# A hybrid encoder layer on one core: order within matmul pairs, a 64-byte start, three first blocks at once, splits ahead of other work

## The chip, the core and the metric

The kernel runs on one core of a Trainium2 chip. TensorE (PE) does the matmuls out of SBUF into PSUM; its weight loads are shown apart as PEld. VectorE (DVE), ScalarE (ACT) and GpSimd (POOL) do the elementwise work, and SyncE (SP) issues nearly all DMAs. The metric is the device time of one execution in microseconds (us), and lower is better.

## The reference, cut to what matters

One layer on 256 tokens of width 2048, in float32:

```
hn   = rmsnorm(x) * norm_w
proj = hn @ w_in                       # 2048 x 18432: q v f_fwd f_bwd z_a b_gate c_gate h_b z_b
A: 16 heads of 128, chunks of 64, forward and backward
   f = lb + (1-lb)*sigmoid(f_logit); k = 1-f; gated linear recurrence of silu(q), k, v
   o_a = head_rmsnorm(o_fwd + o_bwd) * silu(z_a)
B: y = b_gate * conv3(c_gate * h_b);  o_b = rmsnorm(y) * silu(z_b)
h  = x + concat(o_a, o_b) @ w_out      # 4096 x 2048
h  = h + (p @ w_ple) * sigmoid(h @ w_ple_gate)      # 256 x 2048, 2048 x 2048
out = rmsnorm(h)
```

Nearly all arithmetic is in the four matrix products, and all weights are read once.

## The kernel before, in words

**Two halves for precision.** Each float32 operand of a large product is split into a high part, rounded to the matmul's own 32-bit format (fp32r), and the rest, the low part. A product is high x high + high x low + low x high. For weights this is `Stream.split` (L69 on ACT casts the high part, L70 on DVE subtracts it for the low part), for the normalised input `x_split` (L228 on ACT, L229 on DVE), which also multiplies by `norm_w`. The factor 1/rms of each token is applied later, to the results.

**Blocks.** The columns of `w_in` are cut into 72 blocks of 256. One block is a sum over 16 k-tiles of 128 rows, and there are four matmuls in a k-tile: two halves m of the output, and for each a *pair*. The long matmul of a pair has the high part as weights and streams high and low of the other operand, 512 columns, into a whole PSUM bank. The short one has the low part as weights and streams the high part, 256 columns, into the first half of the same bank. In k-tile 0 the pair is issued long, short (L284, L285), since the long one also clears the bank; in the 15 others short, long (L287, L288). The evacuation (`evac`, L302/L303 or L307/L308) adds the two halves of the bank. For blocks of q and the gates the weights are the stationary operand and `xs` (the split input) streams; for `z_a` and `v` it is the other way about (`token_major`).

**Order of blocks.** Pairs of heads i = 0 to 7, each with the blocks FF, FB (forget gates), Q, ZA, V; then i = 0 to 7 with CG, HB, BG, ZB for group B; then the product with `w_out` in four column groups, first the half that has `mixa` as stationary operand (`pa`), then that with `mixb` (`pb`), three matmuls of 512 columns for each k-tile and m (L630 to L632); then `w_ple` (`pp`, stationary `pt`) and `w_ple_gate` (`pg`, stationary `ht`), with the same three lines.

**Weights.** `Stream` loads tiles of 1 MB (`raw`, three buffers) over SP and splits them in halves into `spl` tiles (five buffers). `ws.get(i)` splits up to three parts ahead. A part is four k-tiles of a block.

**Start.** SP issues the first loads by hand (L138 for x, L56 for weights). Blocks FF and FB of pair 0 run together, part by part, and their work on ACT, DVE and PE is kept in the order written (`manual_schedule`). Everything else is ordered by Tile's scheduler: at each point an engine gets, among the instructions it takes to be ready, the one with the highest priority, and priority is the order of the program text. So work of DVE that was written earlier goes ahead of a split written later, if both are ready.

**Norms and attention.** Small steps are placed among the matmuls with `at(dt, fn)`, where one tick is one k-tile of a block. After the first blocks the tokens are loaded row by row into `xf32` (L241), squared and summed (L248 on ACT into a bank with tag `kv`, L249 on DVE into one with tag `o`), turned into 1/rms (`x_norms`, L255 to L259) and spread over partitions by two matmuls (`norms_spread`, L264 to L266: `rps`, `rbc`). POOL multiplies gates and q by `rbc` (L312). `mix_pair` then builds, from the gates, the decays of the recurrence: sigmoid and log on ACT (L376, L379, L386), scans and differences on DVE (L390 to L424), exponentials on ACT (L425 to L428), products on DVE (L429, L430) and on POOL (L438 kc and qc, L444 kx). Scores (L459 and `cx`, L501) and outputs (L511, L512) run on PE 20 to 44 ticks after `mix_pair` is written, that is from the fourth k-tile of the next pair's FF on.

**SBUF.** Pools grow from the left (`const`, `raw`, `spl`, `xs`, and later `ht` in the place of `xs`) and from the right end (`mixa`, below it the attention tiles, later `mixb` in their place). The allocator works in steps of 32 bytes.

Of the kernel before, what the change touches and what calls it, by code (L numbers as in the profile page):

```python
# [8 lines left out]
F32 = mybir.dt.float32  # L9
# [8 lines left out]
P = 128  # L18
# [12 lines left out]
class Stream:  # L31


    def __init__(self, nc, rawp, splp, ahead):
        self.nc, self.rawp, self.splp, self.ahead = nc, rawp, splp, ahead
# [15 lines left out]
    def load(self, j, k0=0, k1=None):  # L51
        src, k, n = self.todo[j]
        if j not in self.raws:
            self.raws[j] = self.rawp.tile([P, 2048], F32, tag="raw", name=f"raw{j}")
        dst = self.raws[j][:, : k * n].rearrange("p (k n) -> p k n", n=n)
        self.nc.sync.dma_start(dst[:, k0:k1], src[:, k0:k1])  # L56
# [24 lines left out]
def tile_hymba_encoder(  # L81
# [26 lines left out]
    mctx = ExitStack()  # L108
    mixp = mctx.enter_context(tc.tile_pool(name="mixp", bufs=1, side="right"))
    mixa = mixp.tile([P, NH, 2, T], F32R, name="mixa")  # L110
    actx = ExitStack()
    ap_ = actx.enter_context(tc.tile_pool(name="ap", bufs=1, side="right"))


    ws = Stream(nc, rawp, splp, 3)
# [18 lines left out]

    xf32 = xp.tile([P, NKT, T], F32, name="xf32")
# [20 lines left out]
    dve.memset(wz, 0.0)  # L156
    wps = psm.tile([P, 512], F32, tag="o", name="wps")
# [76 lines left out]
    rx = const.tile([P, 2], F32, name="rx")  # L234
# [5 lines left out]
    def load_tokens():  # L240
        nc.sync.dma_start(xf32.rearrange("p k t -> p (k t)").rearrange("p (m d) -> p m d", m=2), xtok)  # L241
# [30 lines left out]
    def gemm_part(acc, w, g, token_major):  # L272
        for k in range(4):
            kt = 4 * g + k
            for m in range(2):
                a = acc[m].rearrange("p a b -> p (a b)")
                if token_major:
                    lh, ll = xs[:, kt, 0, m * P : (m + 1) * P], xs[:, kt, 1, m * P : (m + 1) * P]
                    rf, rh = w[:, k, :, :].rearrange("p s n -> p (s n)"), w[:, k, 0, :]
                else:  # L280
                    lh, ll = w[:, k, 0, m * P : (m + 1) * P], w[:, k, 1, m * P : (m + 1) * P]
                    rf, rh = xs[:, kt, :, :].rearrange("p s n -> p (s n)"), xs[:, kt, 0, :]
                if kt == 0:
                    pe.matmul(a, lhsT=lh, rhs=rf, start=True, stop=False)  # L284
                    pe.matmul(a[:, :T], lhsT=ll, rhs=rh, start=False, stop=False)  # L285
                else:
                    pe.matmul(a[:, :T], lhsT=ll, rhs=rh, start=False, stop=False)  # L287
                    pe.matmul(a, lhsT=lh, rhs=rf, start=False, stop=(kt == NKT - 1))  # L288
            tick()
# [25 lines left out]
    ids2 = [blocks[c, 0] for c in (B_FF, B_FB)]  # L315
    acc2 = [acc_in(c, 0) for c in (B_FF, B_FB)]
    with tc.manual_schedule(engines={ENG.Activation, ENG.DVE, ENG.PE}):
        for g in range(4):
            for c in range(2):
                half, v = ws.open(ids2[c][g])  # L320
                if g == 0 and c == 0:
                    for q in range(2):
                        x_split(2 * q)
                        ws.split(half[:, 2 * q : 2 * q + 2], v[:, 2 * q : 2 * q + 2])
                        x_split(2 * q + 1)
                else:
                    if g:
                        x_split(4 * g + 2 * c)
                        x_split(4 * g + 2 * c + 1)
                    ws.split(half, v)  # L330
            for c in range(2):
                gemm_part(acc2[c], ws.parts[ids2[c][g]], g, False)
# [190 lines left out]
    for i in range(8):  # L523
        xf = ap_.tile([P, 2, 2, T], F32, tag="xf", name=f"xf{i}", bufs=2)
        evac(acc2[0] if i == 0 else gemm_in(B_FF, i, False), lambda m: xf[:, 0, m, :], ap_)
        evac(acc2[1] if i == 0 else gemm_in(B_FB, i, False), lambda m: xf[:, 1, m, :], ap_)
        qt = ap_.tile([P, 2, T], F32, tag="qt", name=f"qt{i}")
        evac(gemm_in(B_Q, i, False), lambda m: qt[:, m, :], ap_)
# [61 lines left out]
    rb = const.tile([P, 2], F32, name="rb")  # L590
# [76 lines left out]
    rf = const.tile([P, 2], F32, name="rf")  # L667
    dummy = const.tile([P, 2], F32, name="dummy")
# [118 lines left out]
```

## Time and profile before

| | |
|---|---|
| median of 3 runs | 1159.03 us (1158.61 to 1160.16) |
| the profiled execution | 1158.74 us, span 1157.0 us |
| granted PE clock, mean | 0.995 |
| PE busy | 1142.3 us in 6832 instructions |
| splits on DVE (L70) | 389 instructions, 522.3 us |
| splits on ACT (L69) | 389 instructions, 405.0 us |
| DMA | 214.29 MB, mean 185 GB/s |

The page gives for each engine its busy time and its share of the span. The chain of waits follows the work that ended last back from the last instruction, at each step to what released it. Rows of groups give line, engine, operation, tiles, shape, count, then busy time and mean duration in ns, then the idle time of the engine before them and what ended it. Rows of the timeline give start, duration, engine, line, operation, and in brackets the idle time before and its releaser. Rows of stretches give the busy time of each engine with the number of instructions that touch the stretch, then the granted clock, the DMA share and the GB/s. Ends of matmuls are modelled, so the pace of PE is read from the number of matmuls in a stretch, not from their mean duration.

### The profile page before, as it was taken

The numbers are of one execution on the slowest core, as the hardware profiler recorded it, in microseconds if no ns is written. First come the engines' busy times: TensorE is split into PE (matmuls) and PEld (weight loads), VectorE is DVE, ScalarE is ACT, GpSimd is POOL, SyncE is SP. The second block draws the span as 40 slices with busy tenths as digits, with TensorE's granted clock in tenths as the row PEclk, the third lists the DMA queues.
The fourth block names the chain that finished last, engine by engine and source line by source line (L and its number), as shares of the span: only waits on it lengthen the run. The fifth ranks groups of instructions, "written<-read, shape, count | busy, mean of one in ns | idle before, by whom it ended". The sixth has DMA issues, their size and how long they took to land.

```text
span 1157.0 us, 16851 instructions
## 1 busy us (share of the span) xinstructions
PE 1142.3 (99%) x6832; PEld 981.4 (85%) x6832; DVE 763.6 (66%) x949; ACT 639.9 (55%) x889; POOL 234.8 (20%) x167
## 2 busy tenths in 40 slices
PE   8999999999999999999999999999999999999997
PEld 7878888888888888888888888888888888888886
DVE  6687777685958585966666666676666545545554
ACT  6767576666758584855544444444444334434554
POOL 1232414151414041331221221121210000000121
PEclk9999999999999999999999999999999999999999
DMA  8754545454544555455555555555557555555541
GB/s 284 301 175 153 183 163 196 152 183 146 198 167 159 174 177 181 152 178 182 183 187 184 198 191 187 182 182 184 187 190 262 183 198 180 191 204 196 197 166 74
DMA packets 31614, 214.29 MB, mean 185 GB/s; under 512 B 3504, under 2 KB 3888, under 8 KB 7088
## 3 DMA queue, kind: packets, MB, share of 16 engines
q1 hardware_dynamic: 31392, 213.14, 53.6%
q8 instruction: 53, 0.87, 0.3%
q14 instruction: 25, 0.20, 0.1%
q10 hardware_dynamic: 144, 0.08, 0.0%
HBM read 211.11 MB, written 2.10 MB: 184 GB/s over the span
## 4 chain that ended last, share of the span: by engine, by line
PE 93%; DVE 2%; DMA 2%; POOL 1%; ACT 1%; SPq 0%; issue 0%; ACTq 0%; DVEq 0%
PE a L288 41%; PE a L287 21%; PE a L284 3%; PE pa L630 3%; PE pb L630 3%; PE pb L631 3%; PE pb L632 3%; PE pa L631 3%; PE pa L632 3%; PE pg L630 3%; PE pg L631 3%; PE pg L632 3%; PE a L285 1%; DVE spl L70 1%; PE scps L459 1%; PE cx L501 1%
## 5 line engine op out<-in xcount | busy, mean ns | idle before, releaser
L70 DVE TENSOR_TENSOR spl<-raw,spl 128x1024 fp32r<-128x1024 f32 (+1 forms) x389 | 522.3, 1348 | 305.9 <-ACT spl L69 304.9
L288 PE MATMUL a<-xs,spl 128*128 128x512 f32 x1680 | 597.2, 398 | 0.0
L69 ACT CAST spl<-raw 128x1024 fp32r<-128x1024 f32 (+1 forms) x389 | 405.0, 1045 | 343.0 <-PE a L288 193.7
L287 PE MATMUL a<-xs,spl 128*128 128x256 f32 x1680 | 476.0, 283 | 0.5 <-DVE spl L70 0.3
L288 PEld LDWEIGHTS a<-xs,spl 128*128 128x128 f32 x1680 | 316.7, 189 | 73.0
L287 PEld LDWEIGHTS a<-xs,spl 128*128 128x128 f32 x1680 | 318.1, 189 | 3.7 <-DVE spl L70 1.3
L288 PE MATMUL a<-spl,xs 128*128 128x512 f32 x480 | 171.4, 401 | 2.2 <-DVE spl L70 2.2
L287 PE MATMUL a<-spl,xs 128*128 128x256 f32 x480 | 135.4, 282 | 0.0
L288 PEld LDWEIGHTS a<-spl,xs 128*128 128x128 f32 x480 | 91.0, 190 | 24.1 <-DVE spl L70 2.5
L287 PEld LDWEIGHTS a<-spl,xs 128*128 128x128 f32 x480 | 91.4, 190 | 0.7
L307 ACT COPY r<-a 128x256 f32<-128x256 f32 x112 | 40.6, 372 | 47.4 <-PE a L288 46.8
L691 POOL TENSOR_TENSOR hh<-hh,fw 128x512 f32<-128x512 f32 (+1 forms) x10 | 12.8, 1293 | 264.5 <-PE pp L632 245.0
L630 PE MATMUL pg<-spl,ht 128*128 128x512 f32 (+1 forms) x160 | 55.7, 348 | 0.0
L632 PE MATMUL pg<-spl,ht 128*128 128x512 f32 (+1 forms) x160 | 55.5, 347 | 0.0
L631 PE MATMUL pg<-spl,ht 128*128 128x512 f32 (+1 forms) x160 | 55.5, 347 | 0.0
L630 PE MATMUL pa<-spl,mixa 128*128 128x512 f32 x128 | 51.2, 400 | 0.0
L438 POOL TENSOR_TENSOR qc<-pf,ge 128x256 f32<-128x256 f32 x16 | 43.9, 2748 | 34.4 <-DVE pf L430 34.4
L631 PE MATMUL pb<-spl,mixb 128*128 128x512 f32 x128 | 50.6, 395 | 0.0
L630 PE MATMUL pb<-spl,mixb 128*128 128x512 f32 x128 | 50.6, 395 | 0.0
L632 PE MATMUL pb<-spl,mixb 128*128 128x512 f32 x128 | 50.6, 395 | 0.0
L631 PE MATMUL pa<-spl,mixa 128*128 128x512 f32 x128 | 50.6, 395 | 0.0
L632 PE MATMUL pa<-spl,mixa 128*128 128x512 f32 x128 | 50.6, 395 | 0.0
(174 smaller groups left out, 1233.7 us busy)
## 6 DMA issues: line engine op xcount, KB each, us to landing
raw<-in_w_in_dram SPq DMA_DIRECT2D x140, 1024.0 KB, 5.0
raw<-in_w_out_dram SPq DMA_DIRECT2D x32, 1024.0 KB, 4.9
raw<-in_w_gate_dram SPq DMA_DIRECT2D x12, 1024.0 KB, 4.9
raw<-in_w_gate_end_dram SPq DMA_DIRECT2D x4, 1024.0 KB, 4.9
raw<-in_w_in_dram SPq DMA_DIRECT2D x7, 512.0 KB, 8.4
xf<-in_xtok_dram SPq DMA_DIRECT2D x1, 2048.0 KB, 9.9
hh<-in_xtok_dram SPq DMA_DIRECT2D x1, 2048.0 KB, 8.8
raw<-in_w_ple_dram SPq DMA_DIRECT2D x4, 512.0 KB, 3.5
```

Of the source, the lines that this page charges most:

```text
L69: self.nc.scalar.copy(out=v[:, :, 0, :], in_=r)
L70: self.nc.vector.tensor_tensor(out=v[:, :, 1, :], in0=r, in1=v[:, :, 0, :], op=ALU.subtract)
L284: pe.matmul(a, lhsT=lh, rhs=rf, start=True, stop=False)
L285: pe.matmul(a[:, :T], lhsT=ll, rhs=rh, start=False, stop=False)
L287: pe.matmul(a[:, :T], lhsT=ll, rhs=rh, start=False, stop=False)
L288: pe.matmul(a, lhsT=lh, rhs=rf, start=False, stop=(kt == NKT - 1))
L307: act.copy(out=r, in_=acc[m][:, 1, :])
L438: pool.tensor_tensor(out=c64(dst[:, d]), in0=c64(src[:, d, :, half * P : (half + 1) * P]), in1=g.unsqueeze(3).broadcast_to([P, 2, 2, CH]), ...
L630: pe.matmul(acc[m], lhsT=lh, rhs=w[:, k, 0, :], start=(kt == 0), stop=False)
L631: pe.matmul(acc[m], lhsT=lh, rhs=w[:, k, 1, :], start=False, stop=False)
L632: pe.matmul(acc[m], lhsT=ll, rhs=w[:, k, 0, :], start=False, stop=(kt == nk - 1))
L691: pool.tensor_tensor(out=h, in0=h, in1=fw[:, cs], op=ALU.mult)
```

## The change

1. *Pairs.* `gemm_part` issues long, short in every k-tile.
2. *A start on 64 bytes.* `mixa` gets 8 more elements per partition (32 bytes) and is used without them; all that lies below it on the right side moves by 32 bytes. Four small constants (`rx`, `rb`, `rf`, `dummy`) become slices of one tile `few`.
3. *Three first blocks.* FF, FB and Q of pair 0 run together. Q's sums stand in the banks with tags `kv` and `tr`. The first four k-tiles come in pieces of 1, 1 and 2 k-tiles: loads, splits and matmuls. Second halves of the three weights (tiles `raw1`, `raw3`, `raw5`) go into a pool of their own, `rawx`, in the place where `mixa` is put later. A dummy activation at the start comes ahead of the first real one on ACT. The tokens come in two loads, and the norms' steps at 6 to 14 ticks after the first blocks in place of 18 to 31.
4. *Splits first.* In `get`, splits are issued with a priority as if they were written 300 instructions earlier.

```diff
@@ Stream
+    def load(self, j, k0=0, k1=None, pool=None):
...
+            tag = f"raw{j}" if pool else "raw"
+            self.raws[j] = (pool or self.rawp).tile([P, 2048], F32, tag=tag, name=f"raw{j}")
...
     def get(self, i):
         while self.next <= min(i + self.ahead, len(self.where) - 1):
             if self.next not in self.parts:
-                self.split(*self.open(self.next))
+                part = self.open(self.next)
+                with self.tc.high_priority(offset=300):
+                    self.split(*part)
@@ start
-    mixa = mixp.tile([P, NH, 2, T], F32R, name="mixa")
...
+    rawx = rctx.enter_context(tc.tile_pool(name="rawx", bufs=1, side="right"))
...
+    few = const.tile([P, 16], F32, name="few")
+    rx, rb, rf, dummy = (few[:, 2 * j : 2 * j + 2] for j in range(4))
...
-    load_x(0, 2)
     nc.scalar.dma_start(vec, vecs)
-    ws.load(0, 0, 2)
-    load_x(2, 4)
-    ws.load(0, 2, 4)
-    ws.load(2, 0, 4)
+    PIECES = ((0, 1), (1, 2), (2, 4))
+    for k0, k1 in PIECES:
+        load_x(k0, k1)
+        for c in range(3):
+            ws.load(2 * c, k0, k1)
     for g in range(1, 4):
         load_x(4 * g, 4 * g + 4)
-        for c in range(2):
-            ws.load(2 * c + g // 2, 4 * (g % 2), 4 * (g % 2) + 4)
+        for c in range(3):
+            ws.load(2 * c + g // 2, 4 * (g % 2), 4 * (g % 2) + 4, rawx if g > 1 else None)
...
+    act.activation(dummy[:, 0:1], wz[:, 0:1], AF.Copy)
@@ gemm_part
-                if kt == 0:
-                    pe.matmul(a, lhsT=lh, rhs=rf, start=True, stop=False)
-                    pe.matmul(a[:, :T], lhsT=ll, rhs=rh, start=False, stop=False)
-                else:
-                    pe.matmul(a[:, :T], lhsT=ll, rhs=rh, start=False, stop=False)
-                    pe.matmul(a, lhsT=lh, rhs=rf, start=False, stop=(kt == NKT - 1))
+                pe.matmul(a, lhsT=lh, rhs=rf, start=(kt == 0), stop=False)
+                pe.matmul(a[:, :T], lhsT=ll, rhs=rh, start=False, stop=(kt == NKT - 1))
@@ first blocks
-    ids2 = [blocks[c, 0] for c in (B_FF, B_FB)]
-    acc2 = [acc_in(c, 0) for c in (B_FF, B_FB)]
+    first = (B_FF, B_FB, B_Q)
+    ids3 = [blocks[c, 0] for c in first]
+    acc3 = [acc_in(c, 0) for c in first[:2]]
+    acc3.append([psm.tile([P, 2, T], F32, tag=t, name=f"a{B_Q}_0_{m}") for m, t in enumerate(("kv", "tr"))])
     with tc.manual_schedule(engines={ENG.Activation, ENG.DVE, ENG.PE}):
         for g in range(4):
...
+            parts = [ws.open(ids3[c][g]) for c in range(3)]
+            for k0, k1 in PIECES if g == 0 else ((0, 4),):
+                for k in range(k0, k1):
+                    x_split(4 * g + k)
+                for half, v in parts:
+                    ws.split(half[:, k0:k1], v[:, k0:k1])
+                for c in range(3):
+                    gemm_part(acc3[c], parts[c][1], g, False, k0, k1)
+    rctx.close()
+    mctx = ExitStack()
+    mixp = mctx.enter_context(tc.tile_pool(name="mixp", bufs=1, side="right"))
+    mixa = mixp.tile([P, NH * 2 * T + 8], F32R, name="mixa")[:, : NH * 2 * T]
...
-    at(2, load_tokens)
+    for m in range(2):
+        at(2 + m, lambda m=m: load_tokens(m))
     for c in range(4):
-        at(18 + 2 * c, lambda c=c: x_squares(c))
-    at(27, x_norms)
-    at(31, norms_spread)
+        at(6 + c, lambda c=c: x_squares(c))
+    at(11, x_norms)
+    at(14, norms_spread)
```

More of the change, by code (lines that the diff above doesn't have):

```diff
@@ L232, in x_split @@
         )
-    rx = const.tile([P, 2], F32, name="rx")
     rbc = const.tile([P, T], F32, name="rbc")
@@ L270, in acc_in, with gemm_part @@
         return [psg.tile([P, 2, T], F32, tag="g", name=f"a{c}_{i}_{m}") for m in range(2)]
-    def gemm_part(acc, w, g, token_major):
-        for k in range(4):
+    def gemm_part(acc, w, g, token_major, k0=0, k1=4):
+        for k in range(k0, k1):
             kt = 4 * g + k
@@ L312, in by_norms @@
         pool.tensor_tensor(out=t, in0=t, in1=r.unsqueeze(1).broadcast_to([P, n, T]), op=ALU.mult)
-    ids2 = [blocks[c, 0] for c in (B_FF, B_FB)]
-    acc2 = [acc_in(c, 0) for c in (B_FF, B_FB)]
+    first = (B_FF, B_FB, B_Q)
+    ids3 = [blocks[c, 0] for c in first]
+    acc3 = [acc_in(c, 0) for c in first[:2]]
+    acc3.append([psm.tile([P, 2, T], F32, tag=t, name=f"a{B_Q}_0_{m}") for m, t in enumerate(("kv", "tr"))])
     with tc.manual_schedule(engines={ENG.Activation, ENG.DVE, ENG.PE}):
         for g in range(4):
[L319 to L332, printed above, removed]
+            parts = [ws.open(ids3[c][g]) for c in range(3)]
+            for k0, k1 in PIECES if g == 0 else ((0, 4),):
+                for k in range(k0, k1):
+                    x_split(4 * g + k)
[7 more added lines that the diff above has]
+    mixa = mixp.tile([P, NH * 2 * T + 8], F32R, name="mixa")[:, : NH * 2 * T]
+    mixa = mixa.rearrange("p (k s t) -> p k s t", k=NH, s=2)
+    actx = ExitStack()
+    ap_ = actx.enter_context(tc.tile_pool(name="ap", bufs=1, side="right"))
     at(1, lower_bounds)
-    at(2, load_tokens)
+    for m in range(2):
+        at(2 + m, lambda m=m: load_tokens(m))
     for c in range(4):
-        at(18 + 2 * c, lambda c=c: x_squares(c))
-    at(27, x_norms)
-    at(31, norms_spread)
+        at(6 + c, lambda c=c: x_squares(c))
+    at(11, x_norms)
+    at(14, norms_spread)
     def c64(t):
```

26 lines of the change are left out of this document (9 added, 17 removed).

## The prediction

> **What bounds the kernel now.** I read the page first (busy times, chain of waits), then the busy time by stretches, then the timeline of the first 75 us.
>
> ```profile
> span 1157.0 us, 16851 instructions
> PE 1142.3 (99%) x6832; PEld 981.4 (85%) x6832; DVE 763.6 (66%) x949; ACT 639.9 (55%) x889; POOL 234.8 (20%) x167
> PE 93%; DVE 2%; DMA 2%; POOL 1%; ACT 1%; SPq 0%; issue 0%; ACTq 0%; DVEq 0%
> ```
>
> PE is busy for 99% and carries 93% of the chain. Time can go only where PE waits, where its clock is low, or where the same matmuls follow each other more slowly than they could. Stretches show the first two (columns: stretch, its length, busy time and count of PE, PEld, DVE, ACT, POOL, then granted clock, DMA share, GB/s):
>
> ```profile
> 0.00:7.00 7.00, 4.10 (x21) 3.94 (x21) 1.75 (x7) 2.46 (x4) 3.47 (x18) 1.00 0.67 181
> 7.00:32.50 25.50, 24.90 (x128) 20.56 (x129) 20.19 (x35) 18.65 (x30) 0.00 (x0) 0.93 0.91 334
> 32.50:43.90 11.40, 11.40 (x68) 9.95 (x68) 7.91 (x18) 8.05 (x17) 1.47 (x3) 1.00 0.83 348
> 43.90:55.20 11.30, 11.30 (x68) 10.01 (x67) 7.77 (x10) 7.17 (x10) 4.87 (x2) 1.00 0.80 275
> 55.20:70.30 15.10, 12.89 (x65) 10.97 (x64) 12.67 (x24) 13.85 (x21) 5.29 (x5) 0.89 0.21 73
> ```
>
> The first two blocks (FF and FB of pair 0) end at 32.5, Q at 43.9, ZA at 55.2, V at 70.3. A block is 64 matmuls; V takes 15.1 us, 3.8 more than ZA, at a clock of 0.89. The third kind shows in stretches of PE alone:
>
> ```profile
> 549.69:560.79 11.10, 11.10 (x65) 1.00 0.54 190
> 560.79:572.09 11.30, 11.30 (x66) 1.00 0.54 187
> 594.66:865.54 270.88, 270.88 (x1538) 1.00 0.55 187
> 97.76:131.40 33.64, 33.64 (x193) 1.00 0.51 173
> 918.00:958.00 40.00, 40.00 (x173) 1.00 0.54 184
> 1056.00:1096.00 40.00, 40.00 (x178) 1.00 0.57 197
> ```
>
> Rows 1 and 2 are neighbouring blocks of the same work: 11.10 and 11.30 us, without a wait. Row 3 is 24 blocks at 11.29, row 4 three blocks at 11.21. So one instruction stream has two paces, 347 and 353 ns for a pair of matmuls. Rows 5 and 6 hold only 512-column matmuls, with weights from `mixa`/`mixb` and from `ht`/`pt`; with some two counted at the edges, 40/171 = 234 ns and 40/176 = 227 ns.
>
> **The change, part by part.**
>
> *Padding of mixa.* The 8 extra elements move `mixa` down by 32 bytes, and all that lies below it on that side (`mixb`, the attention tiles). By the tile sizes, in the allocator's steps of 32 bytes, `mixa` and `mixb` start 32 past a multiple of 64 today, `ht` and `pt` on one; after it all four start on one. The moving operand, `spl`, and the shape are the same in rows 5 and 6, so the start of the weights is the candidate for the 7 ns. There are 6 x 128 such matmuls (L630 to L632, `pa` and `pb`, each x128): 768 x 6.7 ns = 5.1 us, all on the path. Bounds 0 to -5.1; I take -5.1, because both stages hold their pace throughout.
>
> Against it speaks the Trainium skill, TensorE: Matmul & The Clock Gate, Step-by-step: what each phase is for: loading the next weights takes no SBUF read bandwidth from the running matmul. By that rule the term is 0 and the forecast 1151; the two rows above do not show that it holds here, but they do not isolate the start address either.
>
> The shared `few` tile makes the other side 64 bytes shorter: `raw`, `spl`, `xs` and `ht` move, and stay on multiples of 64. I cost that at nothing; if starts on 128 mattered, all matmuls would pay, and no row shows one with such a start.
>
> *Long then short.* Today k-tile 0 goes long, short and the others short, long, so a block ends long, the next begins long, and two shorts meet after k-tile 0. Afterwards lengths alternate without a break over all blocks. Matmuls and weight loads are the same in number. The pace changed from 11.10 to 11.30 exactly at a block boundary (560.79), with nothing else on PE, and stayed for the 27 blocks to 865.54. Where no boundary disturbs it, a fast pace could last: 27 x (11.29 - 11.10) = 5 us there, and 21 blocks (Q, ZA, V of seven pairs, row 4) x some 0.15 = 3 us, with a little more in FF and FB: up to -9. If the even alternation locks at the slow pace, the fast ones lose 0.2 each: of 72 blocks 27 and 21 are slow, 14 hold attention matmuls, so some ten, up to +2. The attention matmuls still interrupt and can start either pace, so I take the middle, -4.
>
> *The first three blocks.* Today:
>
> ```profile
> 4.53 1.28 ACT L228 ACT_TABLE_LOAD   x1 [4.53 <-DMA xf<-in_xt_dram]
> 4.65 0.19 DVE L197 TENSOR_TENSOR mx<-vec 128x32 f32<-128x32 f32 x1 [3.00 <-DMA vec<-in_vecs_dram]
> 7.00 0.47 PE L284 MATMUL a<-xs,spl 128*128 128x512 f32 x1 [1.78 <-DVE xs L229]
> 6.46 9.34 SPq L56 DMA_DIRECT2D raw<-in_w_in_dram  x2
> 15.84 0.43 SPq L138 DMA_DIRECT2D xf<-in_xt_dram  x1
> 3.13 8.27 DMA xf<-in_xt_dram
> 4.00:8.00 4.00, 2.07 (x12) 0.99 0.96 263
> 8.00:12.00 4.00, 3.66 (x15) 0.58 1.00 381
> L228 ACT ACTIVATE xs<-xf,vec 128x256 fp32r<-128x256 f32 x16 | 7.4, 501 | 0.2
> L229 DVE SCALAR_TENSOR_TENSOR xs<-xf,vec,xs 128x256 fp32r<-128x256 f32 x16 | 7.1, 480 | 1.2 <-ACT xs L228 1.2
> ```
>
> The dummy activation takes the table load (1.28) out of the wait at 4.53, but `vec`, which x_split also reads, lands only at 4.6. The split of x on ACT and DVE (0.50 and 0.48) puts the first matmul at 5.7, 1.3 earlier. SP issues 24 loads in place of 14, some 0.45 us each by the row at 15.84, done by some 12 us, and no longer stands from 6.5 to 15.8 for a raw buffer, since `rawx` holds the second halves; the weights of ZA and the tokens behind them on SP find it free. Bytes now bind: per k-tile x and three weights, 0.52 MB for 6 x 0.35 = 2.1 us of PE (250 GB/s, against 381 moved at 8 to 12). But the first bytes come slowly: the x load issued at 3.13 landed at 11.4, and with it, in SP's order, 2.1 MB, just k-tiles 0 to 3 of the new order. FF's piece of k-tiles 2 and 3 (1.6 MB) would be there near 10.2 and split by 11.5; 3 x 1.4 us of matmuls end at 15.7, not at 5.7 + 8.4 = 14.1. FF's weights for k-tiles 4 to 7 (3.1 MB, 381 GB/s) land near 14 and are split (ACT 1.05, DVE 1.35, with x in between) by 16.8. Idle together 2.7 us. Three blocks need 3 x 11.1 = 33.3: 5.7 + 2.7 + 33.3 = 41.7, against 43.9. With half the clock somewhere (0.58 at 8 to 12 today) 43.3, with no idle time 39.5. I take -2; bounds -4.4 to 0.
>
> A rule against this part is in the Trainium skill, DMA: Bandwidth & Descriptors, How a descriptor splits into AXI transactions: a descriptor that doesn't start on 256 bytes costs a transaction more, and the shift by 64 takes `raw` and `xf32` off such starts. As an estimate by that page a 1 KB piece then needs 5 for 4, which would take half of these 2 us (forecast 1147), while 8 KB rows lose 3% of a DMA share of 0.54.
>
> *Splits first.* The stall in V:
>
> ```profile
> 36.00 0.70 DVE L249 SCALAR_TENSOR_TENSOR xk<-xf 128x512 f32<-128x512 f32 x1 [1.18 <-DMA xf<-in_xtok_dram]
> 41.31 0.36 DVE L259 COPY rw<-rx 128x128 f32<-128x128 f32 x2
> L264 PE MATMUL rps<-ident,rw 128*128 128x128 f32 x3 | 0.5, 274 | 0.0
> 63.55 0.27 PE L287 MATMUL a<-spl,xs 128*128 128x256 f32 x1
> 66.04 0.80 PE L288 MATMUL a<-spl,xs 128*128 128x512 f32 x1 [2.21 <-DVE spl L70]
> 57.59 0.41 DVE L390 TENSOR_SCALAR xf<-xf,noml,oml 128x256 f32<-128x256 f32 x1 [3.84 <-ACT lf L386]
> 64.76 2.35 DVE L70 TENSOR_TENSOR spl<-raw,spl 128x1024 fp32r<-128x1024 f32 x2
> 50.04 2.63 POOL L312 TENSOR_TENSOR xf<-xf,rbc 128x1024 f32<-128x1024 f32 x1 [9.31 <-DVE rbc L265]
> 72.49 1.91 POOL L444 TENSOR_TENSOR kx<-kc,ge 128x512 f32<-128x512 f32 x1
> 74.45 0.71 PE L501 MATMUL cx<-qc,kx 128*128 128x128 f32 x4 [0.47 <-POOL kx L444]
> L70 DVE TENSOR_TENSOR spl<-raw,spl 128x1024 fp32r<-128x1024 f32 x387 | 520.9, 1352 | 304.8 <-ACT spl L69 303.7
> L69 ACT CAST spl<-raw 128x1024 fp32r<-128x1024 f32 x387 | 403.8, 1047 | 341.8 <-PE a L288 193.7 <-PE pb L632 56.1 <-PE pa L632 47.1
> 126.06 1.05 POOL L444 TENSOR_TENSOR kx<-kc,ge 128x512 f32<-128x512 f32 x1
> 134.76 0.30 PE L459 MATMUL scps<-qc,dd 128*32 128x128 f32 x2
> ```
>
> From 57.6 to 64.8 DVE works on the gates of pair 0 while V's next split waits; PE stands 2.2 us and then runs at half clock: with the clock 4.0 us in all (15.1 - 11.1). Splits ahead of that work end it: -4.0. What is late next is the chain that starts when `rbc` is spread (xf scaled at 50.04) and ends with kx at 74.4, 24.4 us later; today PE arrives just then (0.47). Afterwards PE would be there at 41.9 + 25 = 67 in program order. The chain does not start earlier: the squares of x write into bank `kv`, now held by Q's accumulator until its evacuation after 42. From the squares to `rw` it took 5.7 us today (36.0 to 41.7); with splits between, and `rps` on PE, rbc comes at 50 to 52. More splits (up to 8 x 1.35 for 3 today) then lie within the chain. PE can pass the time with FF of pair 1 if the scheduler orders it so. I net this place at -2; bounds -4 (it does) and +9 (below). For later pairs kx is done at 127 and used at 134.8, 7.7 us of slack against a few splits: nothing. Evacuations wait behind one split, 1.35, of the block of 11 us that PSUM leaves them: nothing. Tokens in two loads: one issue more, hidden.
>
> **Sum.** -5.1 - 4 - 2 - 2 = -13.1 on the profiled execution, 1158.74 us (span 1157.0 and 1.7 around it), 0.3 under the median 1159.03: 1145.6 by its own time, 1146 against the median.
>
> **Rivals.** (1) *The chain to the first scores becomes the bound.* rbc at 52.2, 24.4 us of chain and five more splits, 6.8, give kx at 83.4; PE, if it holds the scores in program order, stands 16 us and one low-clock window, 1.7, follows: 10.4 later than 74.7. With padding -5.1 and order 0, 1164. For it speaks that POOL and DVE already end just in time; against it, that `rps` (L264) ran before 43.9, ahead of ZA's matmuls that the program lists first, so PE's order is not fixed. It decides from kx later than 82 (74.7 + 5.1 + 2.3) where the pace brings nothing.
> (2) *The order brings nothing:* the attention matmuls put PE in the slow pace as before: 1150; with the ten fast blocks lost, 1152. The stretch at 97.76 speaks for it.
> (3) *The padding does nothing* (the pace of `pa` has another cause): 1151.
> (4) *The fast pace holds throughout and V's stall goes whole:* 1159 - 5.1 - 9 - 2 - 4 = 1139.
>
> **How the numbers follow.** Forecast 0.35 (its own range 1142 to 1149), (2) 0.25, (4) 0.15, (1) 0.10, (3) 0.08, between (1) and no change 0.07. Below 1136 lies only (4) with the startup's best end, above 1157 only (1) and its neighbours. 0.2%, 2.3 us, is about what a measurement of this kernel can tell from no change: faster 0.83, same 0.07, slower 0.10.
>
> **What would show it.** `pa` and `pb` at 227 ns spacing (178 in 40 us); blocks at 11.1 us; first matmul by 5.7 and Q's end near 42; V at 11.1 us with no clock below 1 after 12 us; a wait of PE at the first scores under 3 us. I am wrong if PE shows a long wait on POOL kx or DVE before the first scores, if `pa` stays at 173 in 40 us, or if all blocks take 11.3.

## The result, and the profile after

The changed kernel takes 1146.9 us (median of 4 runs, 1145.79 to 1148.26) against 1159.6 us for the kernel before on the same chip (1158.61 to 1160.17). The ratio is 0.9895, with a 95% interval of 0.9883 to 0.9907. The forecast was 1146. The profiled execution took 1148.26 us, against 1158.74 before. The page of the changed kernel, in the three lines that were shown of before:

```profile
span 1146.5 us, 16966 instructions
PE 1130.4 (99%) x6832; PEld 980.6 (86%) x6832; DVE 739.8 (65%) x954; ACT 644.4 (56%) x896; POOL 210.9 (18%) x167
PE 97%; DMA 1%; ACT 1%; POOL 0%; DVE 0%; SPq 0%; issue 0%; ACTq 0%
```

PE does the same 6832 matmuls, 11.9 us of its busy time are gone, and it still carries nearly the whole chain. The start by stretches (columns as in the prediction: stretch, length, busy time of PE, PEld, DVE, ACT, POOL, clock, DMA share, GB/s). The edges are the first matmul, the first of the last 64 of the three blocks, and then the first ones of ZA, of V, and of FF, FB and Q of pair 1:

```profile
5.41:33.56 28.15, 25.91 (x130) 21.06 (x130) 21.36 (x37) 19.15 (x32) 0.00 (x0) 0.94 0.99 367
33.56:44.66 11.10, 11.10 (x67) 9.80 (x66) 6.36 (x8) 5.59 (x9) 0.00 (x0) 1.00 0.84 332
44.66:56.23 11.57, 11.57 (x71) 10.24 (x69) 9.07 (x20) 9.01 (x17) 1.47 (x3) 1.00 0.36 113
56.23:67.53 11.30, 11.30 (x67) 9.82 (x65) 10.46 (x12) 11.13 (x13) 6.07 (x4) 1.00 0.62 228
67.53:78.84 11.31, 11.31 (x67) 9.81 (x65) 10.65 (x19) 9.25 (x13) 0.36 (x1) 1.00 0.64 215
78.84:101.75 22.91, 18.76 (x171) 15.91 (x169) 11.76 (x16) 10.51 (x23) 6.59 (x7) 0.85 0.30 97
```

V (row 4) takes 11.3 us and not 15.1: its stall is gone. But the three blocks end at 44.7 and not before 43.9, and the last row, FB of pair 1 with the scores of pair 0, takes 22.9 us at a clock of 0.85. What PE waits for there, from the waits and the timeline:

```profile
PE cx L508 <- POOL kx L451: 4.1, 1, 4.1
85.50 0.80 PE L508 MATMUL cx<-qc,kx 128*128 128x128 f32 x2 [4.15 <-POOL kx L451]
56.70 2.40 POOL L314 TENSOR_TENSOR xf<-xf,rbc 128x1024 f32<-128x1024 f32 x1 [6.38 <-DVE rbc L271]
83.54 1.91 POOL L451 TENSOR_TENSOR kx<-kc,ge 128x512 f32<-128x512 f32 x1
```

`kx` ends at 85.4, 28.7 us after POOL starts to scale `xf`; before, it ended at 74.4, 24.4 us after. FF and FB of pair 1 together, before and then after:

```profile
70.33:97.76 27.43, 26.95 (x234) 23.58 (x232) 18.31 (x21) 14.39 (x26) 6.36 (x5) 1.00 0.59 196
```

```profile
67.53:101.75 34.22, 30.07 (x235) 25.72 (x233) 22.41 (x34) 19.76 (x35) 6.95 (x8) 0.90 0.42 136
```

Then the long stages, PE alone: of before from Q of pair 1 to the first `pa`, in it the 28 blocks from CG1 on, and `pa` with `pb`:

```profile
97.76:866.34 768.58, 768.58 (x4929) 1.00 0.53 178
549.69:865.54 315.85, 315.85 (x1794) 1.00 0.55 187
866.34:1048.22 181.88, 181.88 (x794) 1.00 0.59 204
```

and the same three of the changed kernel:

```profile
101.75:860.51 758.76, 758.76 (x4930) 1.00 0.53 181
549.09:859.82 310.73, 310.73 (x1796) 1.00 0.56 190
860.51:1037.55 177.04, 177.04 (x794) 1.00 0.60 209
```

From these rows the 10.5 us of the two profiled executions are made up as follows (stretches by the first or last matmul of a block):

| stretch | change, us | forecast |
|---|---|---|
| up to Q of pair 0 (last matmul starts at 43.4, now 44.5) | +1.1 | -2 |
| ZA and V of pair 0 | -3.8 | -4 |
| FF and FB of pair 1, with the scores (27.43 to 34.22) | +6.8 | +2 |
| Q of pair 1 to the end of group B (768.58 to 758.76) | -9.8 | -4 |
| `pa` and `pb` (181.88 to 177.04) | -4.8 | -5.1 |
| the rest | 0 | 0 |
| sum | -10.5 | -13.1 |

So the sum came out near the forecast, but the start lost where it should have gained, the scores lost 4.8 us more than was allowed for them, and the order gained more than twice its term.

### The profile page after: what moved, and what is told of

Same layout as the page of the kernel before. It is cut to its first block, busy times and chain, and to the rows that moved or that the text cites. A ratio compares the mean times of both kernels' runs of the same rounds, so it can differ in the third digit from the quotient of the medians.

```text
span 1146.5 us, 16966 instructions
## 1 busy us (share of the span) xinstructions
PE 1130.4 (99%) x6832; PEld 980.6 (86%) x6832; DVE 739.8 (65%) x954; ACT 644.4 (56%) x896; POOL 210.9 (18%) x167
## 4 chain that ended last, share of the span: by engine, by line
PE 97%; DMA 1%; ACT 1%; POOL 0%; DVE 0%; SPq 0%; issue 0%; ACTq 0%
PE a L289 46%; PE a L290 23%; PE pg L637 3%; PE pg L636 3%; PE pg L638 3%; PE pa L636 3%; PE pa L638 3%; PE pa L637 3%; PE pb L636 3%; PE pb L637 3%; PE pb L638 3%; PE scps L466 1%; PE cx L508 1%; PE o L518 1%; DMA xf<-in_xt_dram 1%; PE o L519 1%
## 5 line engine op out<-in xcount | busy, mean ns | idle before, releaser
L71 DVE TENSOR_TENSOR spl<-raw,spl 128x1024 fp32r<-128x1024 f32 (+2 forms) x394 | 503.7, 1281 | 324.9 <-ACT spl L70 324.4
L289 PE MATMUL a<-xs,spl 128*128 128x512 f32 x1792 | 632.0, 397 | 1.2 <-ACT spl L70 1.2
L70 ACT CAST spl<-raw 128x1024 fp32r<-128x1024 f32 (+2 forms) x394 | 406.6, 1035 | 354.9 <-PE a L290 219.3
L290 PE MATMUL a<-xs,spl 128*128 128x256 f32 x1792 | 501.5, 280 | 1.1 <-DVE spl L71 1.0
L289 PEld LDWEIGHTS a<-xs,spl 128*128 128x128 f32 x1792 | 337.4, 188 | 77.5 <-ACT spl L70 2.1
L290 PEld LDWEIGHTS a<-xs,spl 128*128 128x128 f32 x1792 | 338.9, 189 | 2.4 <-DVE spl L71 2.3
L289 PE MATMUL a<-spl,xs 128*128 128x512 f32 x512 | 178.6, 393 | 0.0
L290 PE MATMUL a<-spl,xs 128*128 128x256 f32 x512 | 143.6, 281 | 0.0
L289 PEld LDWEIGHTS a<-spl,xs 128*128 128x128 f32 x512 | 95.9, 187 | 21.4
L290 PEld LDWEIGHTS a<-spl,xs 128*128 128x128 f32 x512 | 96.9, 189 | 0.0
L637 PE MATMUL pb<-spl,mixb 128*128 128x512 f32 x128 | 49.8, 389 | 0.0
L636 PE MATMUL pb<-spl,mixb 128*128 128x512 f32 x128 | 49.8, 389 | 0.0
L638 PE MATMUL pb<-spl,mixb 128*128 128x512 f32 x128 | 49.8, 389 | 0.0
L504 POOL TENSOR_TENSOR s<-scm 128x256 f32<-128x256 f32 x16 | 17.9, 1121 | 113.1 <-DVE scm L502 113.1
```

The lines of the kernel that those rows point to most:

```text
L70: self.nc.scalar.copy(out=v[:, :, 0, :], in_=r)
L71: self.nc.vector.tensor_tensor(out=v[:, :, 1, :], in0=r, in1=v[:, :, 0, :], op=ALU.subtract)
L289: pe.matmul(a, lhsT=lh, rhs=rf, start=(kt == 0), stop=False)
L290: pe.matmul(a[:, :T], lhsT=ll, rhs=rh, start=False, stop=(kt == NKT - 1))
L504: pool.tensor_tensor(out=s, in0=sm[:, 0:2, :], in1=sm[:, 2:4, :], op=ALU.add)
L636: pe.matmul(acc[m], lhsT=lh, rhs=w[:, k, 0, :], start=(kt == 0), stop=False)
```

## The experiments

### The even order alone

```diff
-                if kt == 0:
-                    ... long, short
-                else:
-                    ... short, long
+                pe.matmul(a, lhsT=lh, rhs=rf, start=(kt == 0), stop=False)
+                pe.matmul(a[:, :T], lhsT=ll, rhs=rh, start=False, stop=(kt == NKT - 1))
```

> The kernel before with one edit: every pair of matmuls is long then short. If the order makes the fast pace (theory A), the blocks from the second pair on fall from 11.28 to 11.08 us each and the time falls by 7 to 10 us, to 1150-1152; V's stall and the first scores stay as they were. If the pace of the changed kernel comes from another part, the padding or the splits (theory B), the blocks stay at 11.28 and the time within 2 us of 1159.

Measured: 1153.92 us, ratio 0.9955 (0.994 to 0.997). From pair 1 to pair 7 the kernel gained 4.7 us, in the last 28 blocks of group B nothing. Q, ZA and V of pair 2, and the 28 blocks from CG1 on:

```profile
157.42:190.84 33.42, 33.42 (x196) 1.00 0.51 171
543.86:860.55 316.69, 316.69 (x1796) 1.00 0.55 186
```

The first row is 11.14 us a block (11.3 before); the second, 316.69 us, is even 0.8 longer than the old order's 315.85, where the changed kernel has 310.73. Theory A holds for the pairs and fails for group B; B fails as well. The even order *can* run at the fast pace, but something else decides whether it does.

### The padding alone

```diff
-    mixa = mixp.tile([P, NH, 2, T], F32R, name="mixa")
+    mixa = mixp.tile([P, NH * 2 * T + 8], F32R, name="mixa")[:, : NH * 2 * T]
+    mixa = mixa.rearrange("p (k s t) -> p k s t", k=NH, s=2)
```

> The kernel before with one edit: mixa has 8 elements more, so that mixa, mixb and the attention tiles start on a multiple of 64 bytes. If the start of the weights sets the pace of pa and pb (theory A), their spacing falls from 234 to 227 ns and the time by 5.0 us, to 1154. If that pace hung on the order of the blocks or on what runs beside them (theory B), 234 ns stays and the time is 1159.

Measured: 1152.89 us, ratio 0.9945 (0.9929 to 0.9962). `pa` and `pb`:

```profile
863.97:1042.57 178.60, 178.60 (x794) 1.00 0.60 207
```

That is 3.3 of the expected 5 us; the spacing within `pb` is 229 ns, not 227. Another 2 us came in the pairs (V1 to CG1), where Q's blocks ran at 346.8 ns a pair of matmuls after 353.1: the attention tiles start 32 bytes lower too, and the blocks after them found another rhythm. It lasts for one block. Q and ZA of pair 2:

```profile
158.69:169.80 11.11, 11.11 (x65) 1.00 0.51 181
169.80:181.09 11.29, 11.29 (x65) 1.00 0.37 112
```

This kernel has the old order of the pairs, and every ZA behind a fast Q is slow. So the padding works, but "a start on 64 bytes" is not the whole of it.

### The splits first, alone

```diff
-                self.split(*self.open(self.next))
+                part = self.open(self.next)
+                with self.tc.high_priority(offset=300):
+                    self.split(*part)
```

> The kernel before with one edit: the splits of later weights go first. V's stall (3.8 us) goes in both theories. If the chain from rbc to the first cx was just in time before (theory A), PE waits for kx instead, by some 4 us and the splits that went ahead, with a window of low clock behind it: 1158 to 1164. If the delay in the changed kernel came from the three blocks at the start, which hold the bank that the squares of x need (theory B), the gain stays: 1155.

Measured: 1159.94 us, ratio 1.0007 (0.9997 to 1.0016): no gain. V of pair 0, and what PE then waits for at the scores:

```profile
56.96:68.07 11.11, 11.11 (x65) 9.72 (x64) 8.21 (x12) 11.02 (x14) 2.74 (x2) 1.00 0.58 190
68.07:98.72 30.65, 27.32 (x234) 23.62 (x233) 21.07 (x32) 17.53 (x33) 7.64 (x7) 1.00 0.43 141
PE scps L462 <- POOL qc L441: 1.7, 1, 1.7
PE scps L462 <- POOL kc L441: 0.8, 1, 0.8
PE cx L504 <- POOL kx L447: 0.8, 1, 0.8
```

V's stall is gone (11.1 us), and FF with FB takes 30.65 us for 27.43: 4.0 gained, 3.2 given back. Theory A, without the window of low clock. This kernel starts with two blocks as before, so the three blocks are not needed for the delay. Between POOL's scaling of `xf` and the end of `kx`, DVE now does ten splits (14.6 us) where it did six (8.3 us), and the chain takes 31.0 us for 24.4.

### The three together, without the three first blocks

```diff
+                pe.matmul(a, lhsT=lh, rhs=rf, start=(kt == 0), stop=False)
+                pe.matmul(a[:, :T], lhsT=ll, rhs=rh, start=False, stop=(kt == NKT - 1))
...
+    mixa = mixp.tile([P, NH * 2 * T + 8], F32R, name="mixa")[:, : NH * 2 * T]
...
+                with self.tc.high_priority(offset=300):
+                    self.split(*part)
```

> The kernel before with order, padding and splits first together, but with its first blocks as they were (two together, whole loads). If the three parts add up, the time is 1159 - 9 - 5 + (the run with splits first alone, less 1159). Against the changed kernel (1147): if the three blocks at the start cost 1.1 us and the late scores 7 (theory A: the bank held by Q's accumulator delays the norms), this kernel is at 1139 to 1141; if the splits are what delays the chain (theory B), at 1146.

Measured: 1148.0 us (1147.35 to 1151.02), ratio 0.9907 (0.989 to 0.9924). Theory B. The three edits alone changed the time by -5.0, -6.0 and +1.0; together they change it by -10.9. Against the changed kernel there is 1.1 us, and 1.6 us of that kernel's lead are in `pa` and `pb` (178.61 against 177.04), so the three first blocks bring nothing that can be seen. Group B is fast in this kernel:

```profile
547.32:858.04 310.72, 310.72 (x1796) 1.00 0.56 190
```

### The scores of pair 0 later

```diff
-            at(20 + 14 * h, lambda h=h: scores(h))
-            at(30 + 14 * h, lambda h=h: outputs(h))
+            late = 24 if i == 0 else 0
+            at(20 + late + 14 * h, lambda h=h: scores(h))
+            at(30 + late + 14 * h, lambda h=h: outputs(h))
```

> The changed kernel with one edit: the scores and outputs of pair 0 are listed 24 k-tiles later, so that PE has matmuls of FB and Q of pair 1 to run until kx is there. If the 4.1 us wait and the low clock behind it (6.8 us at half speed, 3.4 us of work) are both due to PE standing at those scores (theory A), both go and the time falls by 6 to 7.5 us, to 1140. If the low clock has another cause, or the wait only moves to a later instruction (theory B), the gain is 4 us or less: 1143 or more.

Measured: 1141.85 us (1140.88 to 1142.35), ratio 0.985 (0.9835 to 0.9865): 5.0 us faster than the changed kernel. FB and Q of pair 1, in which the scores of pair 0 now lie, and the one wait at scores that is left:

```profile
77.76:103.94 26.18, 26.18 (x226) 22.70 (x225) 19.60 (x24) 18.21 (x30) 11.76 (x8) 1.00 0.47 161
132.85 0.71 PE L508 MATMUL cx<-qc,kx 128*128 128x128 f32 x4 [1.62 <-POOL kx L451]
```

PE does not wait in this stretch any more, and the clock is 1.00: the low clock after 84 us was due to PE standing at those scores, as theory A says. The 1.6 us that are left lie elsewhere, 46 us later, at the scores of pair 1 in FF of pair 2. Their `kx` ends at 132.8; in the changed kernel it ended at 131.0 and was used at 139.5. So moving the scores of pair 0 took the whole slack of the next pair's chain, and part of the wait did move to a later instruction, as theory B has it. The gain, 5.0, lies between the two.

### The norms of x earlier

```diff
-        junk = psm.tile([P, 512], F32, tag="kv", name=f"xj{c}")
-        junk2 = psm.tile([P, 512], F32, tag="o", name=f"xk{c}")
+        junk, junk2 = xr[:, 0, cs], xr[:, 1, cs]
...
                     gemm_part(acc3[c], parts[c][1], g, False, k0, k1)
+        for m in range(2):
+            load_tokens(m)
+        for c in range(4):
+            x_squares(c)
+        x_norms()
...
-    for m in range(2):
-        at(2 + m, lambda m=m: load_tokens(m))
-    for c in range(4):
-        at(6 + c, lambda c=c: x_squares(c))
-    at(11, x_norms)
-    at(14, norms_spread)
+    at(3, norms_spread)
```

> The changed kernel with one edit: the squares of x are taken in place, ahead of Q's evacuation, and not in the bank that Q's accumulator holds; the norms are spread 11 k-tiles earlier. If the chain to the first scores is late because the squares wait for Q's end (theory A), rbc comes 6 to 9 us earlier than 56.6, kx by as much, the wait at cx falls below 1 us and the time by 5 to 7 us, to 1140-1142. If the splits that go first are what stretches the chain (theory B), rbc comes earlier but kx by 2 us at most, and the time falls by 2 us or less.

Measured: 1146.34 us (1144.45 to 1148.53), ratio 0.989 (0.9872 to 0.9909): the changed kernel's time. POOL's scaling of `xf` and its `kx`, and PE's waits at the scores:

```profile
52.41 2.64 POOL L313 TENSOR_TENSOR xf<-xf,rbc 128x1024 f32<-128x1024 f32 x1 [9.45 <-DVE rbc L270]
82.07 1.05 POOL L450 TENSOR_TENSOR kx<-kc,ge 128x512 f32<-128x512 f32 x1
PE scps L465 <- POOL qc L444: 2.0, 1, 2.0
PE scps L465 <- POOL kc L444: 0.8, 1, 0.8
PE cx L507 <- POOL kx L450: 0.8, 1, 0.8
```

The norms are there 4.3 us earlier (52.4 for 56.7), but `kx` ends only 2.3 us earlier (83.1), and PE waits 3.6 us in all. The chain became 30.7 us long, with ten splits in it. Theory B: starting the chain earlier helps little, because the splits go ahead of whichever step of it is ready.

### The order of the pairs as before, all else changed

```diff
-                pe.matmul(a, lhsT=lh, rhs=rf, start=(kt == 0), stop=False)
-                pe.matmul(a[:, :T], lhsT=ll, rhs=rh, start=False, stop=(kt == NKT - 1))
+                if kt == 0:
+                    ... long, short
+                else:
+                    ... short, long
```

> The changed kernel with the order of the pairs as before (long, short in k-tile 0; short, long in the others). If the even alternation carries the whole gain in pace (theory A), the blocks from the second pair on go back to 11.28 us and the time rises by 9 to 10 us, to 1156-1157. If order and gain are only loosely tied, since the same edit alone left the last 28 blocks at 11.20 us, and the entry into those blocks decides (theory B), the rise is 4 to 5 us: 1151-1152.

Measured: 1155.21 us (1154.57 to 1156.67), ratio 0.9967 (0.9955 to 0.9978), 8.3 us above the changed kernel. Group B:

```profile
551.18:867.20 316.02, 316.02 (x1793) 1.00 0.55 187
```

Theory A, a little short of its number: without the even order these 28 blocks take 316.0 us, 5.3 more.

### A larger distance behind mixa

```diff
-    mixa = mixp.tile([P, NH, 2, T], F32R, name="mixa")
+    mixa = mixp.tile([P, NH * 2 * T + 24], F32R, name="mixa")[:, : NH * 2 * T]
```

> The kernel before with 24 elements behind mixa in place of 8: mixa and mixb start 64 bytes lower than with 8. The spacing of pa and pb was 234 ns without padding, 229 with 8 elements alone, 227 in the changed kernel, in which spl starts 64 bytes lower too. If the place of the weights against the moving spl counts (theory A: 0 apart modulo 128 bytes is best), the spacing here is 227 ns. If the start of spl alone makes the last 2 ns, or 64 bytes are all that counts (theory B), it stays at 229.

Measured in one run: 1156.3 us. `pa` and `pb`:

```profile
864.07:1045.74 181.67, 181.67 (x795) 1.00 0.58 204
```

A spacing of 232 to 233 ns, nearly what it was without padding. `mixa` starts on a multiple of 128 here, as `spl` does, and it is *worse* than 64 bytes higher. Both theories fail: neither a start on 64 nor equal places modulo 128 gives 227 ns.

### The same padding in the changed kernel

The four distances so far fit another reading: how far the start of the stationary tile lies from that of `spl`, modulo 512 bytes. This was put to the test with the one edit of 8 to 24 elements.

```diff
-    mixa = mixp.tile([P, NH * 2 * T + 8], F32R, name="mixa")[:, : NH * 2 * T]
+    mixa = mixp.tile([P, NH * 2 * T + 24], F32R, name="mixa")[:, : NH * 2 * T]
```

> The changed kernel with 24 elements behind mixa in place of 8. By the allocator's steps the spacing of pa and pb so far goes with the distance between the start of mixa or mixb and the start of spl, modulo 512 bytes: 32 short of equal 234 ns, 64 short 229, 128 short 232 to 233, equal 227 (the changed kernel). Here mixa starts where it did with 24 elements alone (232 to 233 ns), but spl 64 bytes lower, so that they are 64 short of equal. If the distance counts (theory A), pa and pb come at 229 ns; if the start of the weights by itself counts (theory B), at 232 to 233.

Measured in one run: 1153.87 us, and

```profile
864.63:1043.25 178.62, 178.62 (x795) 1.00 0.60 208
547.23:863.93 316.70, 316.70 (x1796) 1.00 0.54 186
```

178.62 us, 229 ns: theory A, as in the kernel with 8 elements alone (178.60), though `mixa` stands elsewhere. The second row is a surprise: group B is slow (316.70), with the even order and every other part of the change in place.

### Three disturbances in group B

```diff
+    def roll(i):
+        rl = psm.tile([P, 512], F32, tag="o", name=f"rl{i}")
+        for _ in range(i // 2):
+            pe.matmul(rl[:, :P], lhsT=wz, rhs=wz, start=True, stop=True)
...
+        if i in (2, 4, 6):
+            at(4, lambda i=i: roll(i))
```

> The kernel before with the even order (as in the first experiment), and three disturbances on PE: one, two and three 128x128 matmuls on zeros, 4 k-tiles into CG of convolution block 2, 4 and 6; their result is not used. In the first experiment the 28 blocks from CG1 on ran at 352 ns per pair throughout. If PE only keeps the rhythm that its last interruption left (theory A), the pace changes at one or more of the three places, between some 346 and 352 ns, and holds from there to the next. If something of that kernel's layout or loads sets the pace of this stage (theory B), it is 352 ns before and after all three.

Measured in one run: 1154.15 us. The four blocks before CG2, then CG2 with the first disturbance, and the blocks after each of the three:

```profile
543.94:588.31 44.37, 44.37 (x258) 1.00 0.56 190
588.31:599.77 11.46, 11.46 (x68) 1.00 0.56 184
599.77:611.09 11.32, 11.32 (x67) 1.00 0.54 185
690.68:701.98 11.30, 11.30 (x66) 1.00 0.56 186
781.80:793.10 11.30, 11.30 (x66) 1.00 0.54 186
```

11.09 us a block up to the disturbance, 11.3 from the block after it to the end; the second and third changed nothing. Theory A. What is more, the four blocks before it are fast, where the kernel with the same instructions up to there, the first experiment, was slow: even the entry into group B came out differently in two executions.

### The scores of pair 0 later still

```diff
-            late = 24 if i == 0 else 0
+            late = 30 if i == 0 else 0
```

> The changed kernel with the scores and outputs of pair 0 listed 30 k-tiles later in place of 24, which left a wait of 1.6 us on kx. If that wait is only a matter of the place of the scores (theory A), it falls below 0.5 us and the time to 1140; if the chain moves along with PE, since its splits and evacuations share DVE (theory B), 1 to 2 us of wait stay and the time is within 1 us of 1141.9.

Measured: 1139.29 us (1138.63 to 1140.85), ratio 0.9827 (0.9811 to 0.9844). No wait at the scores is left, and this is the fastest kernel of this study, 7.6 us below the changed one. The time is theory A's, but both theories took the 1.6 us for a wait at the scores of pair 0, and it was at those of pair 1. Their `kx` ends at 131.6 here, 1.2 us earlier than with 24 k-tiles, and PE uses it at 132.3; which step of that chain gained is not shown. FF, and FB with Q of pair 1:

```profile
68.45:79.54 11.09, 11.09 (x67) 9.78 (x65) 10.48 (x19) 9.25 (x14) 0.57 (x1) 1.00 0.56 190
79.54:105.24 25.70, 25.70 (x227) 22.56 (x225) 18.67 (x25) 19.12 (x32) 9.25 (x7) 1.00 0.53 173
```

### The same without the splits first

```diff
-                with self.tc.high_priority(offset=300):
-                    self.split(*part)
+                self.split(*part)
```

> The kernel of the run before (scores of pair 0 listed 30 k-tiles later) without the splits first: they stand in the order of the program again. If the splits first are worth V's stall as soon as the scores are out of the way (theory A), the stall comes back, 3 to 4 us with the low clock behind it, and the time is 1142.5 to 1143.5. If they are worth nothing, because the wait moves whatever comes first (theory B), it is within 1 us of 1139.3.

Measured: 1144.05 us (1143.22 to 1144.88), ratio 0.9875 (0.9858 to 0.9893). That is 4.8 us more, a little above theory A. But V of pair 0 runs without a stall here (11.3 us); PE stands in the next block, FF of pair 1. That stretch and its waits:

```profile
66.59:82.51 15.92, 12.81 (x104) 10.33 (x103) 15.53 (x23) 11.45 (x17) 5.68 (x5) 1.00 0.34 113
PE scps L463 <- POOL qc L442: 1.3, 1, 1.3
PE a L287 <- DVE spl L71: 1.0, 1, 1.0
PE scps L463 <- POOL kc L442: 0.8, 1, 0.8
```

3.1 us idle, of which only 1.0 is for a split: with four splits in the chain (23.4 us long) the scheduler put the first scores back into FF, 75 us from the start, though the program lists them later, and PE waits there for kc and qc. So theory A is right on what the splits first are worth beside late scores, and wrong on why: without them the scores don't stay late. Alone, splits first was worth nothing.

## Why the prediction came out

**Padding of mixa (-5.1): right in size, half wrong in cause.** `pa` and `pb` came down by 4.8 us, to 227 ns. But the start on 64 bytes gave 3.3 of it; the other 1.6 came from the shared tile `few`, which moves `spl` by 64 bytes, and which I costed at nothing. What counts is the distance of the stationary tile from `spl` modulo 512 bytes: 0 gives 227 ns, 64 gives 229, 128 gives 232 to 233, 32 gives 234. In the programs as built, `spl` and `mixa` start at 0 and 480 (modulo 512) before, at 0 and 448 with 8 elements alone, 0 and 384 with 24 alone, 448 and 448 in the changed kernel, and 448 and 384 there with 24. `ht` and `pt` start level with `spl` before and after, and run at 227 ns in both. The halves m of the stationary tiles start 512 bytes apart, so no longer period can be meant, but one of 256 would fit these distances as well. That the distance counts, and not a peculiarity of these four, rests on one run that was foretold; why it counts is not shown. The 2 us that the padding gave in the pairs I had not seen at all. The Trainium skill (TensorE: Matmul & The Clock Gate, Step-by-step: what each phase is for) says that loading the next weights takes no read bandwidth from the running matmul. By that rule this term was to be 0, and it was not: the same matmuls took 227 to 234 ns by where the weights lay.

**Long then short (-4, bounds -9 to +2): right in mechanism, mis-sized.** It measured -9.8 from Q of pair 1 to the end of group B, beyond the bound, and 8.3 when it was undone by itself; the padding alone had also brought 2 us in the pairs, so the two shares overlap. A reading behind the bound was off: the stretch 97.76 to 131.40 ends one matmul early. To 131.63 its three blocks take 33.87 us, 11.29 each and not 11.21, so the 21 blocks like them could give 4 us and not 3. I read the two paces in the trace and that boundaries change them, but took the middle for want of a way to say which pace would stay. The runs show more: with the old order, group B was slow in all five kernels that had it (315.85 to 316.02 us for the 28 blocks); with the even order it was fast in six (310.7) and slow in two (316.7), each held from entry to end, and in one it changed at the matmul put in between. All traces together show what the order does. Count, from pair 1 on, the boundaries with no other matmul on PE from the middle of one block to the end of the next. With the old order every fast block was followed by a slow one (26 of 26) and every slow one by a slow one (179). With the even order the pace never changed there (279 times fast, 83 times slow). So the break in the old order ends the fast rhythm at the next block, and the even order keeps whichever it has; the pace is drawn anew only where other matmuls come between. My upper bound, "if the even alternation locks at the slow pace", is what the first experiment did there, and the changed kernel drew the better lot. Which entry leads to which pace stays open.

**The first three blocks (-2, bounds -4.4 to 0): wrong.** The first matmul came at 5.4, as the step said (5.7). The step that failed is the supply of data behind it. The forecast took over the landing times of before: 2.1 MB, which is k-tiles 0 to 3 of all three blocks, by 11.4, and FF's weights for k-tiles 4 to 7 near 14. They landed at 13.0 and at 15.5. Stretches of the changed kernel, and PE's waits for the splits of those last weights:

```profile
5.41:12.00 6.59, 6.33 (x33) 4.88 (x33) 4.26 (x14) 3.77 (x9) 0.00 (x0) 1.00 0.87 230
16.00:19.36 3.36, 1.84 (x9) 1.22 (x8) 2.91 (x5) 2.92 (x3) 0.00 (x0) 1.00 1.03 401
19.36:22.77 3.41, 3.41 (x12) 2.87 (x11) 3.41 (x6) 3.15 (x6) 0.00 (x0) 0.50 1.01 399
22.77:32.50 9.73, 9.73 (x58) 8.59 (x57) 7.42 (x10) 6.34 (x9) 0.00 (x0) 1.00 1.03 419
16.97 0.49 PE L289 MATMUL a<-xs,spl 128*128 128x512 f32 x1 [0.75 <-ACT spl L70]
18.23 0.39 PE L290 MATMUL a<-xs,spl 128*128 128x256 f32 x1 [0.77 <-DVE spl L71]
```

Up to 12 us the DMA moved 230 GB/s at a busy share of 0.87, where the rows of before have 263 (4 to 8 us) and 381 (8 to 12). In the changed kernel the first loads are cut into smaller pieces, but no run isolates that as the cause. Behind the waits the clock was 0.50 for 3.4 us in this execution (third row), which costs 1.7; in the kernel with the scores 24 k-tiles later it stayed at 1.00 up to 32.5 us. From its first matmul to that of ZA the changed kernel takes 39.2 us where three blocks need 33.3: 5.9 us are lost, and the forecast had 2.7. Over all kernels here the last matmul of Q starts at 42.7 to 45.2 us with two first blocks (seven kernels, median 43.4) and at 43.5 to 45.5 with three (seven, median 43.7): no difference beside the spread. By the Trainium skill (DMA: Bandwidth & Descriptors, How a descriptor splits into AXI transactions) a descriptor that does not start on 256 bytes fetches from the boundary below its start. As worded there this is about the side that is read, and the shift by 64 moved only the side that is written. No run isolates it: the 419 GB/s of the same shifted tiles later came in pieces of four k-tiles, 4 KB a row, where the estimate in the prediction would lose little.

**Splits first (-4 for V, net -2): V's stall right, the net wrong.** V's stall went (-3.8). What I named as late next was late: I put `kx` at 83.4 in the first rival, and it ended at 85.4. That rival came true in part: PE did not stand for 16 us, since the scheduler put FF of pair 1 ahead of the scores, but it stood 4.1 us, a low clock followed, and the place cost 6.8 where I had allowed 2. The step that failed is "PE can pass the time with FF of pair 1", which was true for one block only, 4 us too few. By my own list this wait was a sign of being wrong (under 3 us was to be seen), and so was the low clock behind it. The chain also started later than forecast. Rbc came at 56.6, not at 50 to 52: Q ended near 44.7 and not at 41.9, the squares and what follows them took 5.9 us, about as forecast (45.4 to 51.3), and then DVE did four splits, up to 56.3, before it copied `rbc`. Yet with the wait of the squares for Q's evacuation taken away `kx` gained only 2.3 us. The lasting part is DVE's order: nine or ten splits within the chain for six. For the later pairs "7.7 us of slack" was right in the changed kernel (8.5 for pair 1), but the slack was gone once the scores of pair 0 came later.

**The other rivals.** "The padding does nothing" is out. "The order brings nothing" is out for this kernel, but holds for group B in two others with the even order. "The fast pace holds throughout and V's stall goes whole", 1139, is the time of the kernel with the scores 30 k-tiles later, 1139.29, though it counted 2 us for the start that no kernel here shows.

So the total, 0.9 us from the median, owes its closeness to luck: against -13.1 forecast, the scores and the start are 7.9 worse than their terms and the order 5.8 better, and these errors largely cancel.

## What to carry to other kernels

Raising the priority of work that feeds the bottleneck is a trade: name the chain that loses the engine, and move the point where the bottleneck engine needs that chain in the same edit; here the two together gave 4.8 us more than the second alone, while the first alone gave nothing. Moving that point has its own price: look for the wait at the next user of the engines too, which here was the chain of the next pair. When a trace shows two paces of one instruction stream, look for what starts each, and don't take one good run as the pace of the order: an address or an interruption elsewhere can draw the other. And the start of a tile matters against the tile it is read with, not by itself.

## What the runs showed of the hardware that I had not expected

- Alternating matmuls of 512 and 256 columns have rhythms that keep themselves up: start to start some 117 and 230 ns (346.7 for a pair), about 112, 233, 117, 231 over two pairs (also 346.7 a pair), or 113, 233, 117, 241, 120, 236 over three (353.3 a pair). One matmul of 128 columns put in between moved the stream from the second to the third for the rest of the stage.
- Weights and moving operand: 227 to 234 ns for the same matmul of 512 columns, by the distance of their starts (modulo 512 or 256 bytes, which these runs do not tell apart).
- The clock fell to half for a window of 3.4 us without a long wait ahead of it: in the changed kernel PE was busy for 1.84 us of the 3.36 before (stretch 16.00 to 19.36), with no wait above 0.8 us. In the last experiment FF of pair 1 lost 3.1 us in three waits of at most 1.3 us, between 70.0 and 76.9 us, and the clock stayed at 1.00. What decides between the two is not shown.
